# Low-rank inner products moved ahead of the fourth and fifth key tiles, the solve's blocks stored as whole squares, its steps behind the outputs, and another front order on ScalarE

## The chip, the cores and the metric

The kernel runs on one core of one Trainium2 chip. The metric is the device time of one execution in microseconds. Engines: PE (TensorE) multiplies matrices, ACT (ScalarE) evaluates functions and copies, DVE (VectorE) does elementwise work, POOL (GpSimd) does elementwise work and issues DMAs, and SP (SyncE) only issues DMAs. Each engine takes its own instructions in a fixed order; between engines they wait on semaphores.

## The reference, cut to what matters

The program is a two-layer trunk over 512 tokens of width 1024. The change touches only layer 0's time mixing:

```
x_prev = shift(x);  xs = x[None] + (x_prev - x)[None] * mu[:, None, None, :]
r, k, v = einsum('nbtd,nde->nbte', xs[:3], w_rkv)
xw, xa, xg = xs[3], xs[4], xs[5]
w_log = -softplus(-(w0 + tanh(xw @ w1) @ w2)) - 0.5       # low-rank decay
decay = exp(-exp(w_log))
a = sigmoid(a0 + (xa @ a1) @ a2)                          # low-rank rate
g = sigmoid(xg @ g1) @ g2                                 # low-rank gate
kk = k * k_k / |k * k_k|;   k = k * (1 + (a - 1) * k_a)
S = S*w + (S @ -kk)(kk*a)^T + v k^T;  y = S r             # one step per token, 16 heads
```

The layer's channel mixer and the second layer (attention and its channel mixer) follow; they are the same in both kernels.

## The kernel before

The 1024 features lie in eight tiles of 128 partitions, with the 512 tokens in the free dimension. A product of 1024x1024 with the activations is done one output tile (called p) at a time. Each has eight k-steps, and each k-step is three matmuls, since weights and activations are split into a high and a low part: `xh`,`wlo`, then `xl`,`whi`, then `xh`,`whi` (L131 to L135). So one output tile is 24 matmuls of 128x512. A weight arrives by DMA from SP (`wraw`), ACT rounds it to `whi` (L126), and DVE or POOL forms `wlo` (L127).

Time mixing goes through these stages, in this order of code:
- Front: the mean square of x and `rstd` (L145) on ACT as a Ln and an Exp; then `first(k)` per k-step (L434): DVE forms `h`, ACT `hm`, DVE the mixed input, ACT rounds it to `XH[k]`, and DVE forms `XL[k]`.
- Keys (i = 1): `group(1, 0)` runs tiles 0 to 2 with the k-steps interleaved (72 matmuls, `ps_pj`). Then tile 3, the low-rank inner products for k = 0 to 3, tile 4, the inner products for k = 4 to 7 (`inner`, L454), each k with three mixed inputs `lm`, for which ACT makes `lhm`, and three or five plain fp32 matmuls (`ps_l`).
- Low-rank outputs: `hidden` (L401), the gate's sigmoid, then `lora(p)` (L495) beside `group(1, 5)`, which runs tiles 5 to 7. `lora` is four matmuls `ps_lo` and two sigmoids per p.
- Values (i = 2) with `keyed` (L576) in between: `factors` (L516, two Exp per p, `kr` and `ksq`), `key2` (L532, `ps_kn`, Ln and Exp on ACT as `krv`), and `ab` (L542). `ab(p)` makes per chunk and head a 64x64 block and writes it to DRAM as `s_ab`, with two POOL DMAs. Its tile comes from a pool of three buffers with the tag `sq`, shared with `ksq` and `krv`.
- Receptances (i = 0) and the solve: `solve` (L609) loads the triangular 32x32 blocks from `s_ab`, does 31 elimination steps on DVE for the first four chunks (g = 0) and 31 for the last four (g = 1), and writes the inverses to `s_xd` and `s_x1`. `steps(n)` puts n of them at a place in the code, and `fetch_x(ch)` (L653) reads what chunk ch needs.
- The loop over eight chunks (L869): `u_step`, `u2_step`, `scores`, `s_step`, `tokens`, `y_tokens`, `yt`, `inv1`, `inv2`.

A scheduler orders each engine's instructions from the code's order and from priorities (`tc.high_priority`, which weights and solve steps use). `preload_act_table_set` (L94) loads an ACT function table at a fixed place; where a function's table isn't loaded, a load is put in front of it (`ACT_TABLE_LOAD` without that line).

Of the kernel before, what the change touches and what calls it, by code (L numbers as in the profile page):

```python
# [31 lines left out]
SM_SCALE = 1.0 / math.sqrt(96.0)  # L32
LOG_EXP = "natural_log_exp_and_others"
HALF = (slice(0, 64), slice(64, 128))
# [21 lines left out]
class Trunk:  # L56
# [23 lines left out]
    def act(self, out, in_, func=AF.Copy, **kw):  # L80
        self.nc.scalar.activation(out=out, in_=in_, func=func, **kw)  # L81

# [9 lines left out]

    def use_log_exp(self):
        self.tc.keep_in_program_order(self.nc.scalar.preload_act_table_set(LOG_EXP))  # L94

# [49 lines left out]
    def rstd(self, out, ss, n, ps=None):  # L145

        if ps is None:
            ss = ss if isinstance(ss, list) else [ss]
            ps = self.bank("ps_ss")[:, :ss[0].shape[1]]
            for i, s in enumerate(ss):  # L150
                self.nc.tensor.matmul(ps, lhsT=self.ones, rhs=s, start=i == 0, stop=i == len(ss) - 1)  # L151
        self.act(out, ps, AF.Ln, scale=1.0 / n, bias=self.eps)
        self.act(out, out, AF.Exp, scale=-0.5)


    def run(self):
# [4 lines left out]
        dp = self.open("scratch", space=DRAM)  # L161
        self.s_ab = dp.tile([2, DT, 4, P, C], F32, name="s_ab")
        self.s_xd = dp.tile([2, P, D], F32, name="s_xd")
# [143 lines left out]
    def time_mix(self, nxt, cp, gt):  # L307
# [21 lines left out]
        x = self.x  # L329
        self.use_log_exp()  # L330

# [15 lines left out]
        rs = t1.tile([P, T], F32, tag="en", name="rs")  # L347
        self.rstd(rs, None, D, ps)
        def mix(i, k):
            hm = tp.tile([P, T], F32, tag="hm", name="hm", bufs=1)  # L350
            self.act(hm, h[:, k, 1:], AF.Copy, scale=om[:, 8 * i + k:8 * i + k + 1])
            m = tp.tile([P, T], F32, tag="xs", name="xs")
            self.stt(m, h[:, k, 0:T], V("mu", 8 * i + k), hm, ALU.mult, ALU.add)
            self.act(XH[k], m)
            return k, m
# [9 lines left out]

        def group(i, p0, pre=None, prio=GP, mid=None):

            lag = LAG
            w = [self.weight(I["wrkv"][i, p], prio=prio) for p in range(p0, p0 + 3)]
            q = [self.bank("ps_pj") for _ in range(3)]  # L370
            pend = None
            for k in range(DT + 1):
                n = pre(k) if pre and k < DT else k
                if k:
                    if pre:
                        mix_lo(*pend)
# [64 lines left out]

        qk = group(1, 0, first, prio=G0)
        for t, n in ((w1, I["w1"]), (g1, I["g1"]), (self.cst, I["cst"][:, :256]), (self.ident, I["cst"][:, 256:]), (scan, I["scan"])):
# [10 lines left out]
        def inner(k):  # L454
            lm = []
            for i, tag in enumerate(("xs", "be", "kr")):
                hm = tp.tile([P, T], F32, tag="sq", name="lhm", bufs=3)
                self.act(hm, h[:, k, 1:], AF.Copy, scale=om[:, 8 * (3 + i) + k:8 * (3 + i) + k + 1])
                m = tp.tile([P, T], F32, tag=tag, name="lm", bufs=3 if tag == "kr" else None)
                self.stt(m, h[:, k, 0:T], V("mu", 8 * (3 + i) + k), hm, ALU.mult, ALU.add)  # L460
                lm.append(m)
# [33 lines left out]
        def lora(p):  # L495
            if p == DT:
                return
# [6 lines left out]

        qk = group(1, 5, mid=lora)
        for p in range(5, DT):
            kept(p, qk[p - 5])
        self.use_log_exp()

# [6 lines left out]
        def factors(p):  # L516
            cp = cs[:, p, :]
            en = t1.tile([P, T], F32, tag="en", name="en")
            self.act(en, cp, AF.Exp, scale=CD)
            ka = t1.tile([P, T], F32, tag="ka", name="ka")  # L520
            nc.vector.tensor_scalar(out=c3(ka), in0=bk[:, p, :, 0, :], scalar1=V("ka", p), scalar2=om[:, 48 + p:49 + p], op0=ALU.mult, op1=ALU.add)
            self.act(ar[:, p, :, 1, :], c3(cp), AF.Exp, scale=-CD)
            self.tt(ka, ka, en, ALU.mult)
# [77 lines left out]
        LT, X1 = (s4[:, 1].rearrange("q (i p) (o c) -> q i (p o) c", i=2, o=2)[:, i] for i in range(2))  # L601
        abv = self.s_ab.rearrange("g p c (h b j) t -> (g p c h) b j t", h=2, b=2)
        tmp = {"tm": t1.tile([P, 256], F32, tag="ke", name="tm")}

        def load_a(g, A):
            for b in range(2):
                nc.sync.dma_start(out=A[b * 64:b * 64 + 64], in_=abv[g * 64:g * 64 + 64, b, :, b * 32:b * 32 + 32])

        def solve():  # L609
            nc.sync.dma_start(out=lA, in_=abv[:, 0, :, 32:64])  # L610
            load_a(0, sA)
            nc.vector.tensor_copy(out=lX, in_=lA.rearrange("q j i -> q i j"))
            nc.gpsimd.dma_start(out=self.s_lo, in_=lX.rearrange("q a b -> q (a b)"))
# [255 lines left out]
        for ch in range(NCH):  # L869
# [4 lines left out]
            if ch == 0:  # L874
# [71 lines left out]
class FFN:  # L946
# [25 lines left out]
    def run(self, nxt):  # L972
# [11 lines left out]
        for j in range(FT):  # L984
# [358 lines left out]
```

## Time and profile before

| | us |
|---|---|
| median of 3 runs (range) | 1341.83 (1340.74 to 1344.11) |
| the profiled execution | 1340.55 |
| its span, first to last instruction | 1338.8 |
| PE busy | 1294.0 (97%) |
| DVE busy | 807.5 (60%) |
| ACT busy | 695.8 (52%) |
| POOL busy | 250.9 (19%) |

Between its span and its time lie 1.75 us. Busy time is an average over stages with different limits; a stage has to be read by itself. The mean granted TensorE clock is 0.992 of full speed.

### The profile page before, as it was taken

What the parts mean: (1) busy time and instruction counts of PE and PEld (TensorE: products, weight loads), DVE (VectorE), ACT (ScalarE), POOL (GpSimd) and SP (SyncE); (2) the same over time, 40 slices, a digit from 0 to 9 for tenths busy, and PEclk for the clock granted to TensorE, in tenths of its full rate; (3) what the DMA queues carried; (4) which work ended last, traced back from release to release, by engine and by line L of the source; (5) the groups of instructions that cost most, each with busy time, mean ns of one, the idle gap of its engine ahead of it and who ended that gap; (6) DMA issues with size and microseconds to landing.
All of it is one profiled execution on the core that took longest, in us unless ns stands there. A gap on an engine that the chain in (4) does not pass through costs nothing.

```text
span 1338.8 us, 21742 instructions
## 1 busy us (share of the span) xinstructions
PE 1294.0 (97%) x8120; PEld 1063.4 (79%) x8120; DVE 807.5 (60%) x1458; ACT 695.8 (52%) x1313; POOL 250.9 (19%) x237
## 2 busy tenths in 40 slices
PE   7999999989999999999999999999999999999996
PEld 4566687878998888888888978677988888888886
DVE  7669787977787666665233877873765555550003
ACT  6699744677765444443332566664664444433221
POOL 0001423000000000000000051203154444444440
PEclk8999999999999999999999999999999999999998
DMA  6222595344633323333333145332323332333321
GB/s 208 67 73 84 153 259 142 62 121 119 200 108 127 101 96 95 101 96 87 95 95 95 57 113 122 96 83 64 96 95 103 100 96 95 100 93 90 96 79 64
DMA packets 111084, 141.41 MB, mean 106 GB/s; under 512 B 47553, under 2 KB 54593, under 8 KB 110977
## 3 DMA queue, kind: packets, MB, share of 16 engines
q1 hardware_dynamic: 107568, 129.52, 33.3%
q0 software_dynamic: 3408, 10.49, 2.5%
q8 instruction: 64, 1.05, 0.3%
q14 instruction: 44, 0.35, 0.1%
HBM read 120.31 MB, written 12.58 MB: 99 GB/s over the span
## 4 chain that ended last, share of the span: by engine, by line
PE 72%; DVE 6%; ACT 3%; DMA 1%; issue 1%; SPq 0%; ACTq 0%; DVEq 0%
PE ps_in L134 12%; PE ps_in L135 12%; PE ps_in L133 12%; PE ps_out L133 7%; PE ps_out L135 7%; PE ps_out L134 7%; PE ps_o L1205 2%; PE ps_t L1189 1%; PE ps_wo L133 1%; PE ps_wo L135 1%; PE ps_wo L134 1%; PE ps_ss L151 1%; PE ps_dn L134 1%; PE ps_dn L135 1%; PE ps_dn L133 1%
## 5 line engine op out<-in xcount | busy, mean ns | idle before, releaser
L81 ACT ACTIVATE whi<-wraw 128x512 fp32r<-128x512 f32 (+2 forms) x411 | 249.3, 614 | 358.6 <-PE ps_out L135 129.1
L127 POOL TENSOR_TENSOR wlo<-wraw,whi 128x512 fp32r<-128x512 f32 (+2 forms) x168 | 211.9, 1266 | 690.6 <-ACT whi L81 680.1
L133 PE MATMUL ps_in<-xh,wlo 128*128 128x512 f32 (+1 forms) x768 | 286.2, 373 | 0.2 <-DVE wlo L127 0.2
L135 PE MATMUL ps_in<-xh,whi 128*128 128x512 f32 (+1 forms) x768 | 285.3, 372 | 0.0
L134 PE MATMUL ps_in<-xl,whi 128*128 128x512 f32 (+1 forms) x768 | 285.3, 371 | 0.0
L127 DVE TENSOR_TENSOR wlo<-wraw,whi 128x512 fp32r<-128x512 f32 x237 | 160.0, 682 | 108.8 <-ACT whi L81 106.9
L133 PEld LDWEIGHTS ps_in<-xh,wlo 128*128 128x128 f32 x768 | 144.6, 188 | 25.5 <-DVE wlo L127 0.4
L134 PEld LDWEIGHTS ps_in<-xl,whi 128*128 128x128 f32 x768 | 144.6, 188 | 25.4 <-DVE xl L87 0.2
L135 PEld LDWEIGHTS ps_in<-xh,whi 128*128 128x128 f32 x768 | 144.6, 188 | 24.8
L133 PE MATMUL ps_out<-hh,wlo 128*128 128x512 f32 (+1 forms) x396 | 146.8, 371 | 1.3 <-ACT mg L81 1.3
L134 PE MATMUL ps_out<-hl,whi 128*128 128x512 f32 (+1 forms) x396 | 146.2, 369 | 0.0
L135 PE MATMUL ps_out<-hh,whi 128*128 128x512 f32 (+1 forms) x396 | 146.2, 369 | 0.0
L84 DVE TENSOR_TENSOR macc<-macc,msq 128x512 f32<-128x512 f32 (+1 forms) x25 | 15.7, 626 | 126.7 <-ACT msq L81 126.6
L133 PEld LDWEIGHTS ps_out<-hh,wlo 128*128 128x128 f32 x396 | 74.3, 188 | 16.2 <-ACT mg L81 1.9
L87 DVE SCALAR_TENSOR_TENSOR c<-gp,vec,c 128x512 f32<-128x512 f32 x88 | 71.5, 815 | 24.4 <-ACT c L81 23.1
L133 PE MATMUL ps_pj<-xh,wlo 128*128 128x512 f32 x192 | 77.8, 424 | 8.7 <-ACT xh L81 6.7
L135 PEld LDWEIGHTS ps_out<-hh,whi 128*128 128x128 f32 x396 | 74.3, 188 | 14.2
L134 PEld LDWEIGHTS ps_out<-hl,whi 128*128 128x128 f32 x396 | 74.3, 188 | 14.2
L134 PE MATMUL ps_pj<-xl,whi 128*128 128x512 f32 x192 | 77.7, 406 | 0.1
L135 PE MATMUL ps_pj<-xh,whi 128*128 128x512 f32 x192 | 76.8, 402 | 0.0
L84 DVE TENSOR_TENSOR u<-ps_in,row 128x512 f32<-128x512 f32 x44 | 30.4, 690 | 64.1 <-PE ps_in L135 64.1
L84 DVE TENSOR_TENSOR gp<-ps_in,row 128x512 f32<-128x512 f32 x44 | 30.4, 691 | 60.3 <-PE ps_in L135 49.7
(293 smaller groups left out, 2277.6 us busy)
## 6 DMA issues: line engine op xcount, KB each, us to landing
wraw<-in_win SPq DMA_DIRECT2D x176, 256.0 KB, 2.7
wraw<-in_wout SPq DMA_DIRECT2D x80, 256.0 KB, 2.6
wraw<-in_wrkv SPq DMA_DIRECT2D x48, 256.0 KB, 3.0
wraw<-in_wo SPq DMA_DIRECT2D x32, 256.0 KB, 3.0
x<-in_xT SPq DMA_DIRECT2D x16, 256.0 KB, 4.6
wraw<-in_ow SPq DMA_DIRECT2D x16, 256.0 KB, 3.0
s_ab<-ab POOLq DMA_DIRECT2D x16, 128.0 KB, 2.5
s_vt<-vT POOLq DMA_DIRECT2D x8, 256.0 KB, 3.2
```

The source lines that it names most:

```text
L81: self.nc.scalar.activation(out=out, in_=in_, func=func, **kw)
L84: self.nc.vector.tensor_tensor(out=out, in0=a, in1=b, op=op)
L87: self.nc.vector.scalar_tensor_tensor(out=out, in0=a, scalar=s, in1=b, op0=op0, op1=op1)
L127: self.wlo.tensor_tensor(out=l[:, :w], in0=r, in1=h[:, :w].bitcast(F32), op=ALU.subtract)
L133: mm(ps, lhsT=wl, rhs=xh, start=start, stop=False)
L134: mm(ps, lhsT=wh, rhs=xl, start=False, stop=False)
L135: mm(ps, lhsT=wh, rhs=xh, start=False, stop=stop)
L151: self.nc.tensor.matmul(ps, lhsT=self.ones, rhs=s, start=i == 0, stop=i == len(ss) - 1)
L1189: nc.tensor.transpose(out=q[:, o:o + P], in_=pr[i][:, j * P:(j + 1) * P], identity=t.ident)
L1205: nc.tensor.matmul(q[HALF[i], j * P:], lhsT=VT[pr // 4][j][:, c:c + 64], rhs=w, start=j == 0, stop=j == QB - 1)
```

## The change

1. `use_log_exp` becomes `use_table(name)`, which also loads the sigmoid table. The sigmoid table is loaded behind the inner products. The two Exp of `factors` are held behind the later load of the Ln/Exp table.
2. All eight `inner(k)` stand directly behind the first three key tiles. Tiles 3 and 4 follow, then `lora(0)` and `lora(1)`, then `group(1, 5)` with `lora(k + 2)`.
3. In the front, the weights of key tiles 1 and 2 are issued behind `rstd`'s Exp, and `lhm` is held behind the second `XH`.
4. `s_ab` has the two 32-column halves outermost, so that a 32x32 block is contiguous: four POOL DMAs for each p with rows of 128 B, where there were two with rows of 256 B. The solve's loads read contiguous 4 KB per partition instead of 32 pieces of 128 B. Their order changes, and the transposing copy of the off-diagonal blocks (`lX`) moves from DVE to ACT.
5. In the chunk loop, `steps` are 10, 10, 10 behind `yt` (they were 11, 11, 40 ahead of `y_tokens`), and the rest stands behind chunk 3's `u2_step`. `fetch_x(n)` moves from the end of one round to behind the next round's `u2_step`.

```diff
-        qk = group(1, 0, first, prio=G0)
+        qk = group(1, 0, first, prio=G0, after=normed)
...
-                self.act(hm, h[:, k, 1:], AF.Copy, scale=om[:, 8 * (3 + i) + k:8 * (3 + i) + k + 1])
+                with tc.issue_after(rounded[1].ins):
+                    self.act(hm, h[:, k, 1:], AF.Copy, scale=om[:, 8 * (3 + i) + k:8 * (3 + i) + k + 1])
...
-        for p in range(3, 5):
-            kept(p, proj(1, p))
-            for k in range(4):
-                inner(4 * (p - 3) + k)
+        for k in range(DT):
+            inner(k)
+        kept(3, proj(1, 3))
...
+        self.use_table(SIGMOID)
...
-        qk = group(1, 5, mid=lora)
+        q4 = proj(1, 4)
+        for p in range(2):
+            lora(p)
+        kept(4, q4)
+        qk = group(1, 5, mid=lambda k: lora(k + 2))
...
-        self.use_log_exp()
+        exps = self.use_table()
...
+            with tc.issue_after(exps.ins):
+                self.act(en, cp, AF.Exp, scale=CD)
...
             for g in range(2):
-                nc.gpsimd.dma_start(out=self.s_ab[g, p].rearrange("c q t -> q c t"), in_=c3(o)[:, 4 * g:4 * g + 4])
+                for b in range(2):
+                    nc.gpsimd.dma_start(out=self.s_ab[b, g, p].rearrange("c q t -> q c t"), in_=c3(o)[:, 4 * g:4 * g + 4, 32 * b:32 * b + 32])
...
-            nc.sync.dma_start(out=lA, in_=abv[:, 0, :, 32:64])
             load_a(0, sA)
-            nc.vector.tensor_copy(out=lX, in_=lA.rearrange("q j i -> q i j"))
+            nc.sync.dma_start(out=lA, in_=abv[1, :, 0])
+            self.act(lX, lA.rearrange("q j i -> q i j"))
...
             u2_step(ch, u)
+            if ch == 3:
+                steps(40)
+            if 0 < ch and n < NCH:
+                fetch_x(n)
...
-            if ch < 3:
-                steps((11, 11, 40)[ch])
             y_tokens(ch, q)
             if ch > 0:
                 yt(ch - 1)
+            if ch < 3:
+                steps(10)
...
-            if n + 1 < NCH:
-                fetch_x(n + 1)
```

How the instructions stand on the engines follows at three places. First ACT's order in the front, from `rstd`'s Ln (`rs<-ps_x`) to the first rounded key input `xh`; `whi` are rounded weights. Before:

```order
L81 ACTIVATE rs<-ps_x,eps 128x512
L81 ACTIVATE whi<-wraw 128x512 x2
L81 ACTIVATE rs<-rs 128x512
L81 ACTIVATE hm<-h,om 128x512
L81 ACTIVATE whi<-wraw 128x512 x2
L81 ACTIVATE lhm<-h,om 128x512
L81 ACTIVATE xh<-xs 128x512
```

With the change, the same stretch as far as the second `xh`:

```order
L81 ACTIVATE rs<-ps_x,eps 128x512
L81 ACTIVATE rs<-rs 128x512
L81 ACTIVATE whi<-wraw 128x512 x2
L81 ACTIVATE hm<-h,om 128x512
L81 ACTIVATE whi<-wraw 128x512
L81 ACTIVATE xh<-xs 128x512
L81 ACTIVATE whi<-wraw 128x512
L81 ACTIVATE hm<-h,om 128x512
L81 ACTIVATE xh<-xs 128x512
```

Two roundings moved behind the Exp, and one rounding behind the first `xh` and the `lhm` behind the second.

Next ACT's order where the Ln/Exp table is loaded (`ACT_TABLE_LOAD` of L94), at the end of the keys; `bk<-ps_pj` is `kept`, `en` an Exp, and `ksq` what `ps_kn` multiplies. Before:

```order
L81 ACTIVATE bk<-ps_pj 128x8x64
L94 ACT_TABLE_LOAD
L81 ACTIVATE en<-cs 128x512
L81 ACTIVATE kr<-bk,vec 128x512
L81 ACTIVATE ksq<-bk,vec 128x512
L81 ACTIVATE xh<-xs 128x512
```

With the change, the first `kr` and `ksq` stand among the sigmoids `sg` and `bk<-ps_lo`, 24 rows ahead of that load:

```order
L81 ACTIVATE bk<-ps_lo,vec 128x8x64
L81 ACTIVATE kr<-bk,vec 128x512
L81 ACTIVATE sg<-ps_lo,vec 128x512
L81 ACTIVATE bk<-ps_lo,vec 128x8x64
L81 ACTIVATE ksq<-bk,vec 128x512
L81 ACTIVATE sg<-ps_lo,vec 128x512
```

So `kr` and `ksq` of p = 0 no longer follow the table load.

Last POOL's order over the last writes of `s_ab` (p = 3 to 7); `s_v` and `s_vt` are the values. Before:

```order
L551 DMA s_ab<-ab 128x4x64 x2
L432 DMA s_v<-vv 128x4x128
L423 DMA s_vt<-vT 128x512
L551 DMA s_ab<-ab 128x4x64 x2
L432 DMA s_v<-vv 128x4x128
L551 DMA s_ab<-ab 128x4x64 x6
```

With the change:

```order
L564 DMA s_ab<-ab 128x4x32 x3
L436 DMA s_v<-vv 128x4x128
L564 DMA s_ab<-ab 128x4x32
L427 DMA s_vt<-vT 128x512
L564 DMA s_ab<-ab 128x4x32 x4
L436 DMA s_v<-vv 128x4x128
L564 DMA s_ab<-ab 128x4x32 x12
```

POOL issues four writes for each p where it issued two, and twelve in a row at the end where there were six.

## Rows read from the trace of the kernel before

**Rows 1.** The page: PE's busy tenths in 40 slices of the span

```profile
PE   7999999989999999999999999999999999999996
```

**Rows 2.** Stretches: length, busy PE, PEld, DVE, ACT, POOL, PEclk, DMA, GB/s

```profile
10.00:20.00 10.00, 3.72 (x9) 1.74 (x8) 8.03 (x15) 8.08 (x14) 0.00 (x0) 0.87 0.87 298
20.00:30.00 10.00, 9.76 (x34) 7.02 (x32) 9.29 (x16) 5.26 (x10) 0.00 (x0) 0.78 0.23 79
30.00:70.00 40.00, 39.75 (x148) 20.14 (x148) 27.51 (x43) 28.35 (x46) 0.00 (x0) 1.00 0.22 67
70.00:100.00 30.00, 27.68 (x115) 20.72 (x113) 21.34 (x28) 29.68 (x48) 0.00 (x0) 1.00 0.25 79
100.00:110.00 10.00, 8.20 (x25) 5.79 (x26) 9.24 (x16) 10.00 (x18) 0.00 (x0) 0.83 0.07 26
...
160.00:230.00 70.00, 69.54 (x372) 54.75 (x371) 59.24 (x128) 31.99 (x51) 19.24 (x32) 1.00 0.72 200
230.00:350.00 120.00, 110.59 (x2048) 100.48 (x2045) 93.69 (x199) 81.92 (x184) 1.67 (x4) 0.99 0.46 118
600.00:620.00 20.00, 20.00 (x90) 16.54 (x89) 12.22 (x19) 7.64 (x12) 0.00 (x0) 1.00 0.33 89
```

**Rows 3.** PE's waits to 400 us: line, released by: total us, times, longest

```profile
PE ps_pj L133 <- ACT xh L81: 6.7, 2, 6.3
...
PE ps_kn L534 <- ACT ksq L81: 2.4, 1, 2.4
PE ps_ab L547 <- ACT krv L81: 2.3, 1, 2.3
PE ps_i L669 <- DMA s<-s_xd: 2.3, 1, 2.3
```

**Rows 4.** ACT in time in the front: start, us, instruction, idle before it

```profile
12.78 1.14 ACT L81 ACTIVATE whi<-wraw 128x512 fp32r<-128x512 f32 x2
...
15.42 0.72 ACT L81 ACTIVATE hm<-h,om 128x512 f32<-128x512 f32 x1 [0.99 <-DVE h L87]
16.05 1.13 ACT L81 ACTIVATE whi<-wraw 128x512 fp32r<-128x512 f32 x2
...
17.71 0.61 ACT L81 ACTIVATE xh<-xs 128x512 fp32r<-128x512 f32 x1
```

**Rows 5.** PE in time: end of the inner products, first `ps_kn`, first `ps_ab`

```profile
69.27 1.05 PE L470 MATMUL ps_l<-lm,ar 128*32 128x512 f32 x4
...
101.80 1.12 PE L534 MATMUL ps_kn<-ksq,cst 128*128 128x512 f32 x2 [2.43 <-ACT ksq L81]
...
116.73 0.56 PE L547 MATMUL ps_ab<-ar,bk 64*64 64x64 f32 x10
```

**Rows 6.** ACT in time: one table load between neighbours, and the first `krv`

```profile
77.05 0.63 ACT L81 ACTIVATE gs<-gs 32x512 f32<-32x512 f32 x1
77.70 1.28 ACT L81 ACT_TABLE_LOAD   x1
79.00 0.63 ACT L81 ACTIVATE ar<-cs 128x512 f32<-128x512 f32 x1
...
112.32 0.61 ACT L81 ACTIVATE krv<-krv 128x512 f32<-128x512 f32 x1
```

**Rows 7.** POOL in time: the first, fourth and last pair of `s_ab` writes

```profile
121.12 1.69 POOL L551 DMA_DIRECT2D s_ab<-ab  x2 [119.15 <-ACT ab L81]
...
145.81 1.49 POOL L551 DMA_DIRECT2D s_ab<-ab  x2 [0.35 <-ACT ab L81]
...
163.06 1.49 POOL L551 DMA_DIRECT2D s_ab<-ab  x2 [2.16 <-ACT ab L81]
```

**Rows 8.** ACT in time: the wait for an `s_ab` landing

```profile
150.45 0.69 ACT L81 ACTIVATE krv<-ps_kn,tiny 128x512 f32<-128x512 f32 x1 [2.20 <-DMA s_ab<-ab]
```

**Rows 9.** DMA issues: queue, count, KB each, median us to landing

```profile
s_ab<-ab POOLq DMA_DIRECT2D x16, 128.0 KB, 2.5
...
s<-s_ab SPq DMA_DIRECT2D x4, 256.0 KB, 4.4
```

More of the change, by code (lines that the diff above doesn't have):

```diff
@@ L32 @@
 SM_SCALE = 1.0 / math.sqrt(96.0)
-LOG_EXP = "natural_log_exp_and_others"
+LOG_EXP, SIGMOID = "natural_log_exp_and_others", "sigmoid_and_others"
 HALF = (slice(0, 64), slice(64, 128))
@@ L80, in act @@
     def act(self, out, in_, func=AF.Copy, **kw):
-        self.nc.scalar.activation(out=out, in_=in_, func=func, **kw)
+        return self.nc.scalar.activation(out=out, in_=in_, func=func, **kw)
     def tt(self, out, a, b, op):
@@ L91, in split, with use_table @@
         self.tt(lo, src, hi.bitcast(F32), ALU.subtract)
-    def use_log_exp(self):
-        self.tc.keep_in_program_order(self.nc.scalar.preload_act_table_set(LOG_EXP))
+    def use_table(self, name=LOG_EXP):
+        return self.tc.keep_in_program_order(self.nc.scalar.preload_act_table_set(name))
     def bank(self, nm):
@@ L152, in rstd @@
         self.act(out, ps, AF.Ln, scale=1.0 / n, bias=self.eps)
-        self.act(out, out, AF.Exp, scale=-0.5)
+        return self.act(out, out, AF.Exp, scale=-0.5)
     def run(self):
@@ L161, in run @@
         dp = self.open("scratch", space=DRAM)
-        self.s_ab = dp.tile([2, DT, 4, P, C], F32, name="s_ab")
+        self.s_ab = dp.tile([2, 2, DT, 4, P, 32], F32, name="s_ab")
         self.s_xd = dp.tile([2, P, D], F32, name="s_xd")
@@ L329, in time_mix @@
         x = self.x
-        self.use_log_exp()
+        self.use_table()
         warm = bank2("ps_w")
@@ L347, in time_mix @@
         rs = t1.tile([P, T], F32, tag="en", name="rs")
-        self.rstd(rs, None, D, ps)
+        normed = self.rstd(rs, None, D, ps)
+        rounded = []
         def mix(i, k):
@@ L353, in mix @@
             self.stt(m, h[:, k, 0:T], V("mu", 8 * i + k), hm, ALU.mult, ALU.add)
-            self.act(XH[k], m)
+            rounded.append(self.act(XH[k], m))
             return k, m
@@ L364, in proj, with group @@
             return q
-        def group(i, p0, pre=None, prio=GP, mid=None):
+        def group(i, p0, pre=None, prio=GP, mid=None, after=None):
             lag = LAG
-            w = [self.weight(I["wrkv"][i, p], prio=prio) for p in range(p0, p0 + 3)]
+            w = [self.weight(I["wrkv"][i, p0], prio=prio)]
+            with tc.issue_after(after.ins) if after else ExitStack():
+                w += [self.weight(I["wrkv"][i, p], prio=prio) for p in range(p0 + 1, p0 + 3)]
             q = [self.bank("ps_pj") for _ in range(3)]
@@ L495, in lora @@
         def lora(p):
-            if p == DT:
+            if p >= DT:
                 return
@@ L503, in lora @@
             self.act(bk[:, p, :, 0, :], c3(q), AF.Sigmoid, bias=V("a0", p))
-        qk = group(1, 5, mid=lora)
+        q4 = proj(1, 4)
[3 more added lines that the diff above has]
+        qk = group(1, 5, mid=lambda k: lora(k + 2))
         for p in range(5, DT):
             kept(p, qk[p - 5])
-        self.use_log_exp()
+        exps = self.use_table()
         def before(p):
@@ L518, in factors @@
             en = t1.tile([P, T], F32, tag="en", name="en")
-            self.act(en, cp, AF.Exp, scale=CD)
+            with tc.issue_after(exps.ins):
+                self.act(en, cp, AF.Exp, scale=CD)
             ka = t1.tile([P, T], F32, tag="ka", name="ka")
             nc.vector.tensor_scalar(out=c3(ka), in0=bk[:, p, :, 0, :], scalar1=V("ka", p), scalar2=om[:, 48 + p:49 + p], op0=ALU.mult, op1=ALU.add)
-            self.act(ar[:, p, :, 1, :], c3(cp), AF.Exp, scale=-CD)
+            with tc.issue_after(exps.ins):
+                self.act(ar[:, p, :, 1, :], c3(cp), AF.Exp, scale=-CD)
             self.tt(ka, ka, en, ALU.mult)
@@ L601, in time_mix @@
         LT, X1 = (s4[:, 1].rearrange("q (i p) (o c) -> q i (p o) c", i=2, o=2)[:, i] for i in range(2))
-        abv = self.s_ab.rearrange("g p c (h b j) t -> (g p c h) b j t", h=2, b=2)
+        abv = self.s_ab.rearrange("b g p c (h a j) t -> b (g p c h) a j t", h=2, a=2)
         tmp = {"tm": t1.tile([P, 256], F32, tag="ke", name="tm")}
@@ L606, in load_a @@
             for b in range(2):
-                nc.sync.dma_start(out=A[b * 64:b * 64 + 64], in_=abv[g * 64:g * 64 + 64, b, :, b * 32:b * 32 + 32])
+                nc.sync.dma_start(out=A[b * 64:b * 64 + 64], in_=abv[b, g * 64:g * 64 + 64, b])
         def solve():
-            nc.sync.dma_start(out=lA, in_=abv[:, 0, :, 32:64])
             load_a(0, sA)
-            nc.vector.tensor_copy(out=lX, in_=lA.rearrange("q j i -> q i j"))
+            nc.sync.dma_start(out=lA, in_=abv[1, :, 0])
+            self.act(lX, lA.rearrange("q j i -> q i j"))
             nc.gpsimd.dma_start(out=self.s_lo, in_=lX.rearrange("q a b -> q (a b)"))
@@ L1004, in run @@
             ls.append(b)
-        t.use_log_exp()
+        t.use_table()
         mp = t.open("mg")
```

## The prediction

> **What bounds the kernel now.** I read the page's slices first. PE is at 9 tenths in nearly every slice [rows 1], and in the stretch 600:620 it is busy for all 20 us with 90 matmuls, so one costs 20/90 = 0.222 us there [rows 2]. From about 400 us on nothing but fewer matmuls could shorten the program, and the change takes no matmul away. So I cut the first 400 us into stretches [rows 2]. PE is short of work in the front (3.72 of 10 us), in 70:100 (27.68 of 30), in 100:110 (8.20 of 10) and in the chunk loop, 230:350 (110.59 of 120). ACT has no time left where PE is short: 29.68 of 30 us in 70:100, 10.00 of 10 in 100:110. That is the stage of the low-rank outputs and their sigmoids. The granted clock falls to 0.83 in 100:110, and to 0.87 and 0.78 in the two front stretches, which is the lower level (1.2 of 2.4 GHz) for a part of each, behind PE's longest stops. PE's waits give the names [rows 3]: the first `xh` (6.3 us), `ksq` (2.4 us, in front of the first `ps_kn` at 101.80 [rows 5]), `krv` (2.3 us), and the fetch from `s_xd` for chunk 4 (2.3 us).
>
> **The front.** The change lets 1.14 us of rounding (the two `whi` at 12.78) follow the Exp instead of standing ahead of it [rows 4]. `hm` at 15.42 had waited 0.99 us for `h`, which needs that Exp, so the 1.14 counts in full. Behind `hm` one of two roundings (half of 1.13, so 0.57) and an `lhm` (the 0.53 between the end of those roundings at 17.18 and `xh` at 17.71) move behind `xh`. Together 2.24 us. Against it, DVE now has two `wlo` between `h` and the mixed input; with the front's DVE rows (9.29 us busy for 16 instructions, 0.58 each [rows 2]) they cost up to 1.16. That leaves about 1.1, and PE starting earlier also shortens the stretch at the lower clock a little: I take -1.3 us. The bounds are 0 (DVE, at 9.29 of 10, hands the loss to the later k-steps) and -3: the 2.24 in full and part of the 2.2 us that a clock of 0.78 over 20:30 costs.
>
> **The inner products in one piece.** Their own time I leave as it is: in 30:70, where before's stand with a key tile between the halves, PE is busy 39.75 of 40 us, ACT 28.35 and DVE 27.51 [rows 2], so PE paces them. The cover for `lm` is now the inner products alone. A miss here would cost up to 1 us; I take 0.
>
> **From the end of the inner products to the first `ps_ab`.** This carries the forecast. Before, it runs from 69.27 + 1.05 = 70.3 to 116.73 [rows 5], 46.4 us, in which PE does 127 key and value matmuls and 32 `ps_lo`. With the change tiles 3 and 4 also stand behind the inner products, and the first `ps_ab` stands two matmuls earlier: 173 and 32, so 46 more. Had they been done elsewhere at full pace, before would take 46.4 + 46 x 0.222 = 56.6 us for the same work. If PE is the limit, the changed stretch takes 205 x 0.222 = 45.5, and 1.1 for the two first `ps_kn` [rows 5], so 46.6 us: a gain of 10.0. If ACT is the limit, its new order has 60 operations and three table loads as far as the last key tile's `kept`, and 12 operations and one load from there to the first `krv`'s Exp. An operation takes 0.56 us: 29.68 less three loads of 1.28 and the 0.96 of a fourth that began before 70, over the other 45 [rows 2, 6]. So 72 x 0.56 + 4 x 1.28 = 45.4. Behind it DVE needed 3.8 us, from the end of the first `krv`'s Exp at 112.93 [rows 6] to `ps_ab` at 116.73 [rows 5]. That makes 49.2 us: a gain of 7.4. The two limits are close, and ACT's is the later one. I take -7.4. The wait for `ksq` and the lower clock in 100:110 are inside it: `ksq` now stands ahead of the table load, so it is early, and what is late next is `krv` in front of the first `ps_ab`, priced by ACT's sum. As bounds I take -10.0, and -4 if ACT in addition idles as DVE's or PE's turn comes (it then gains only the 2.4 us wait, its 1.7 us of lost clock and nothing in 70:100).
>
> The row on the table load [rows 6]: the operation ahead of it ends at 77.68, the load starts at 77.70 and takes 1.28, and the next operation starts at 79.00. The Trainium skill ("ScalarE: Activation LUTs", section "What ACT_TABLE_LOAD costs") adds a drain of 1.38 us to such a load, 2.66 in all. By that the four loads would cost ACT 5.5 us more, and the gain of the stretch would be 1.9. By the row, which shows no drain, it is 7.4; the sum goes by the row.
>
> **`s_ab` as squares.** Each p now has four writes from POOL; a pair took 1.49 us [rows 7], so the last write starts 1.5 us later. That is hidden where `ab` tiles are rare, and before's pairs come (163.06 - 121.12)/7 = 6.0 us apart on average [rows 7], later ones closer. It isn't hidden at the fourth: written at 145.81, it held ACT's `krv` for 2.20 us until 150.45 [rows 7, 8], and PE's wait of 2.3 us for `krv` follows from that [rows 3]. So I take +1.5, once. Bounds: 0, if ACT and PE come there later by their own work, and +3, if the wait behind the fifth tile's writes adds the same again. In exchange the solve's loads have whole rows; they took 4.4 us in 128 B pieces [rows 9]. DVE's first solve steps now stand ahead of the last `xl` of the receptances, so sooner loads are needed there; in 160:230 PE is busy 69.54 of 70 us and has no loss to give back [rows 2]. The moved transposing copy goes to ACT, busy 31.99 of those 70: nothing.
>
> The Trainium skill ("DMA: Bandwidth & Descriptors", section "Specifications") says that transfers below 512 B leave the line rate, since they are done as read-modify-write. By it the new 128 B writes would land later than the 256 B ones, whose median is 2.5 us [rows 9]. The nearest row of 128 B pieces is the solve's load, 4.4 us for four times the bytes of a new write [rows 9]; by the bytes a write is then no later than before, and the sum keeps 1.5.
>
> **The chunk loop.** The solve's last step for the later chunks stands three DVE operations further back; at 93.69/199 = 0.47 us each [rows 2] that is 1.4 us on the way to `s_xd` and to PE's wait of 2.3 us [rows 3]. The solve's faster start works the other way. I take +0.5, bounds -2.3 (the wait goes) and +2. Fetching later changes nothing for chunks 1 to 3, whose blocks are long in DRAM; for chunks 4 and on SP waited for `s_xd` anyway.
>
> **The sum.** -1.3 - 7.4 + 1.5 + 0.5 = -6.7 us. The profiled execution took 1340.55: its span 1338.8 and 1.75 around it. So 1333.85 in its terms; the median of the runs is 1.28 higher, and the forecast is 1335.1.
>
> **The rivals.** A: ACT stays the bound and the gain is mostly used up. The low-rank stretch gives only 4, the front 0.5, and the squares take 2.5 (their bound nearly): -2.0, and 1339.8. For it: ACT at 29.68 and 10.00, and its new order holds more operations as far as `kept` than PE's matmuls cover. The table load's drain, by the page named above, would end here too (1.9 - 1.5 - 0.5 + 1.3 = 1.2 us gained). Against it: the row shows no drain. B, slower: the squares pace the stage. One `ab` copy (0.56), four issues (3.0) and a landing (2.5) make 6.1 us from one tile to the next, against the 6.0 on average before; with a landing like the fourth's (145.81 + 1.49 to 150.45, so 3.15 us) 6.7. If the chain holds PE's order over all seven steps from one tile to the next, each later by the 1.5 us of issues and by the 0.65 that such a landing takes longer, this costs 7 x 2.15 = 15.1 us; the front and the low-rank stretch give 8.7, the loop loses 0.5: +6.9, 1348.7. It decides once every write takes over 3 us to land. Against it: before's first pairs have more room than the last ones. C: PE is the limit throughout, -2 - 10.0 + 0.5 for the squares and 0 for the loop: -11.5, 1330.3. For it: ACT and PE lie only 2.6 us apart in my sums, and the earlier start of the sigmoids may carry over to the later tiles.
>
> **How the numbers follow.** I give the forecast 0.50, with a range of its own of 1332 to 1338.5, A 0.23, B 0.10, C 0.17. What a measurement tells from no change is 0.3%, 4.0 us: faster is below 1337.8, slower above 1345.9. Nine tenths of the forecast, all of C and a little of A lie below: 0.64. The rest of the forecast, the most of A and some of B lie between: 0.27. Slower is 0.09. The range that should hold 8 in 10 goes from 1329.5 (C and half a microsecond) to 1343 (A, and the squares' other bound and the loop's on top); it leaves out B and the tails.
>
> **What would show it.** In the changed profile the first `xh` should start near 16.4 instead of 17.71. The first `ps_kn` should wait for nothing, and the granted clock should stay at 1.00 from there to the first `ps_ab`. From the end of the inner products to that `ps_ab` it should be about 49 us; 54 or more means rival A. One of ACT's operations should wait longer than 2.2 us for `s_ab`, and PE's wait for `krv` should grow to 3 or 4 us; waits at several tiles mean B. PE's wait for `s_xd` should be 2 to 4 us. I am wrong at the root if PE's loss in the low-rank stretch is not ACT's doing: if ACT shows idle time there and PE still waits.

## The result and the profile after

The changed kernel takes 1350.27 us (median of 5 runs, 1347.03 to 1350.97), the kernel before beside it on the same chip 1340.74 (median of 5, 1338.59 to 1344.11). The ratio is 1.0067, with a 95% interval of 1.0053 to 1.0082: slower, where a gain of 6.7 us was forecast, and outside the range. The profiled execution took 1349.0, its span 1347.2.

The stretches of the changed kernel, to be laid beside [rows 2] (same columns):

```profile
10.00:20.00 10.00, 5.19 (x12) 2.65 (x11) 7.88 (x15) 6.98 (x12) 0.00 (x0) 0.75 0.92 313
20.00:30.00 10.00, 9.51 (x36) 6.90 (x36) 9.84 (x17) 7.49 (x14) 0.00 (x0) 0.90 0.20 67
30.00:70.00 40.00, 40.00 (x144) 18.91 (x143) 29.37 (x47) 32.63 (x51) 0.00 (x0) 1.00 0.17 53
70.00:100.00 30.00, 28.41 (x123) 22.43 (x122) 24.27 (x32) 29.14 (x51) 0.00 (x0) 1.00 0.31 101
100.00:110.00 10.00, 9.99 (x41) 7.23 (x39) 9.72 (x17) 9.90 (x19) 0.00 (x0) 1.00 0.20 71
110.00:130.00 20.00, 17.59 (x151) 12.96 (x152) 16.16 (x29) 15.86 (x35) 6.59 (x9) 1.00 0.27 70
130.00:160.00 30.00, 25.07 (x191) 18.88 (x192) 18.82 (x31) 19.82 (x37) 16.69 (x24) 0.94 0.54 145
160.00:230.00 70.00, 66.51 (x347) 52.68 (x349) 55.35 (x121) 31.61 (x48) 22.19 (x34) 0.98 0.67 199
230.00:350.00 120.00, 108.08 (x2002) 97.04 (x2002) 91.58 (x196) 79.64 (x175) 4.24 (x8) 0.96 0.42 103
```

Two stretches of the kernel before that were not looked at ahead of the prediction:

```profile
110.00:130.00 20.00, 19.46 (x132) 14.56 (x132) 19.05 (x32) 18.72 (x35) 3.87 (x6) 1.00 0.30 94
130.00:160.00 30.00, 27.14 (x258) 20.24 (x257) 22.02 (x36) 23.60 (x49) 12.58 (x18) 1.00 0.53 158
```

Up to 110 us the change does what it was forecast to do: PE gains in 10:20 and 70:110, and the clock of 0.83 in 100:110 is 1.00. Behind that PE, DVE and ACT are all less busy than before in 110:160, which points to something that isn't an engine. PE alone is busy 1.87 + 2.07 us less there, 3.03 less in 160:230 and 2.51 in 230:350, and its mean granted clock is lower from 130 us on (0.94, 0.98 and 0.96 in the last three stretches). PE's longest waits up to 420 us name the later places:

```profile
PE ps_i L682 <- DMA s<-s_xd: 6.2, 1, 6.2
PE ps_pj L133 <- ACT xh L81: 5.3, 3, 4.8
PE ps_ab L558 <- DVE bk L84: 5.2, 2, 2.9
PE ps_bo L709 <- DVE rkk L87: 3.5, 1, 3.5
```

Against [rows 3] the wait for `ksq` is gone and the first is 1.5 us shorter; the wait for `s_xd` has grown from 2.3 to 6.2, and two names are new.

To see where each microsecond goes I compared when the same matmul (the n-th onto a named tile) starts in two traces. Start minus its start in the kernel before, us; the experiments' columns are described below. `ps_vt` belongs to the values, `ps_bo` to the receptances (it multiplies `rkk`, their product with the keys), `ps_sc` to the loop's scores, and `ps_ss` is the first matmul behind the loop:

| matmul | before, at | after | old blocks (e1) | old steps (e2) | both old (e3) |
|---|---|---|---|---|---|
| first `ps_pj` | 18.37 | -1.3 | -2.0 | -1.3 | -1.2 |
| last inner product `ps_l` | 69.73 | -9.7 | -10.4 | -9.7 | -9.6 |
| first `ps_ab`, p = 0 | 116.73 | -5.9 | -6.6 | -4.5 | -5.8 |
| first `ps_ab`, p = 6 | 157.18 | +2.7 | -7.3 | +4.6 | -6.3 |
| last `ps_vt` | 183.62 | +0.4 | -8.2 | +2.4 | -7.2 |
| last `ps_bo` | 226.99 | +5.1 | -6.7 | +4.1 | -4.9 |
| `ps_sc` of chunk 4 | 273.56 | +5.1 | -4.8 | +4.8 | -5.6 |
| first `ps_ss`, past the wait for `s_xd` | 361.34 | +9.0 | -0.8 | +4.0 | -4.8 |

(The last inner product is early because 48 key matmuls now stand behind it.) So the changed kernel arrives at the key/value outputs 5.9 us ahead and loses in three places: 8.6 us between the outputs of p = 0 and p = 6, 4.7 from the last `ps_vt` to the last `ps_bo` of the receptances, and 3.9 at chunk 4's wait for `s_xd`.

The table also shows how far a single trace can be trusted. The changed kernel and e2 run the same instructions in the same order on each engine as far as 260 us, e1 and e3 as far as 250 us, and yet each pair differs by up to 2 us in a row up to there. The first loss is far above that: 8.6 and 9.1 us (e2), where e1 and e3 gain 0.7 and 0.5. The second is not: 4.7 in the changed kernel, but 1.8 in e2, and 1.5 and 2.3 with the old blocks.

**The first place.** POOL and ACT of the changed kernel in time, at the first two tiles (as [rows 7, 8]):

```profile
116.50 3.46 POOL L564 DMA_DIRECT2D s_ab<-ab  x4 [114.53 <-ACT ab L81]
...
127.98 3.00 POOL L564 DMA_DIRECT2D s_ab<-ab  x4 [0.97 <-ACT ab L81]
```

```profile
123.98 0.69 ACT L81 ACTIVATE krv<-ps_kn,tiny 128x512 f32<-128x512 f32 x1 [3.74 <-DMA s_ab<-ab]
...
133.54 0.69 ACT L81 ACTIVATE krv<-ps_kn,tiny 128x512 f32<-128x512 f32 x1 [1.46 <-DMA s_ab<-ab]
```

`ab` and `krv` share three buffers. The four issues begin at 116.50 and the `krv` that takes a buffer next isn't written until 123.98, 7.5 us later: 2.7 until the fourth issue begins, and 4.7 until that write has landed (the median of all these writes is 2.7). Before, the only such wait came at the fourth pair [rows 8]; now the first tile has one, and what stands behind `krv` inherits it: DVE's `bk`, and PE, which waits 2.24 and 2.02 us:

```profile
128.21 1.15 PE L558 MATMUL ps_ab<-ar,bk 64*64 64x64 f32 x32 [2.24 <-DVE bk L84]
...
134.28 1.86 PE L433 MATMUL ps_vt<-cen,vT 128*128 128x128 f32 x8 [2.02 <-ACT krv L81]
```

**The second place.** ACT, DVE and PE of the changed kernel at the first receptance:

```profile
177.91 2.04 ACT L81 ACTIVATE s<-s 128x1024 f32<-128x1024 f32 x1 [1.45 <-DMA s<-s_ab]
```

```profile
180.50 0.69 DVE L84 TENSOR_TENSOR xl<-xs,xh 128x512 fp32r<-128x512 f32 x1 [2.37 <-ACT xh L81]
...
192.51 0.42 DVE L84 TENSOR_TENSOR s<-s,tm 128x252 f32<-128x252 f32 x1
192.85 0.68 DVE L84 TENSOR_TENSOR ar<-ps_pj,ar 128x512 f32<-128x512 f32 x1
...
194.65 0.75 DVE L87 SCALAR_TENSOR_TENSOR rkk<-ar,vec,bk 128x512 f32<-128x512 f32 x1
```

```profile
195.54 1.61 PE L709 MATMUL ps_bo<-rkk,cst 128*128 128x512 f32 x2 [3.49 <-DVE rkk L87]
```

DVE takes its work in order, and the solve's steps stand ahead of the product `ar`: 18 of them here, two operations each, where the kernel before has 13 and the old blocks 12. Twelve of the 18 also start late: DVE stood idle for 2.37 us until ACT had made the last `xh`, and ACT had first waited 1.45 us for the load of the moved transposing copy (`s<-s`) and copied for 2.04. PE stops for 3.49 us and then runs partly at the lower clock: the two `ps_bo` take 1.61 (1.10 before), and the granted clock is 0.83 in 190:200.

**The third place.** The solve's last step reaches POOL, and PE, so late:

```profile
284.74 0.57 POOL L642 DMA_DIRECT2D s_xd<-s  x1 [48.99 <-issue]
```

```profile
294.17 1.12 PE L682 MATMUL ps_i<-s 128*64 128x64 f32 x16 [6.19 <-DMA s<-s_xd]
```

Before, that write was issued at 276.81.

### The profile page after: what moved, and what is told of

It reads as the page before. It is cut to its first block, busy times and chain, and to the rows that moved or that the text cites. A ratio compares the mean times of both kernels' runs of the same rounds, so it can differ in the third digit from the quotient of the medians.

```text
span 1347.2 us, 21781 instructions
## 1 busy us (share of the span) xinstructions
PE 1297.6 (96%) x8120; PEld 1066.6 (79%) x8120; DVE 806.7 (60%) x1457; ACT 696.8 (52%) x1313; POOL 263.2 (20%) x253
## 4 chain that ended last, share of the span: by engine, by line
PE 71%; DVE 3%; ACT 2%; DMA 1%; issue 1%; SPq 0%; POOL 0%; ACTq 0%; POOLq 0%; DVEq 0%
PE ps_in L134 12%; PE ps_in L135 12%; PE ps_in L133 12%; PE ps_out L133 7%; PE ps_out L135 7%; PE ps_out L134 7%; PE ps_o L1220 1%; PE ps_wo L133 1%; PE ps_wo L135 1%; PE ps_wo L134 1%; PE ps_t L1204 1%; PE ps_ss L151 1%; PE ps_dn L134 1%; PE ps_dn L135 1%; PE ps_dn L133 1%
```

## The experiments

Ratios are to the kernel before, run beside each on the same chip, with 95% intervals.

### Which part costs: blocks and steps undone apart and together

Theory S lays the loss on the square blocks, theory L on the steps behind the outputs. e1 puts the old `s_ab` with its two writes, its loads and the copy on DVE back into the changed kernel; e2 the old place of the steps and of the fetch; e3 both.

```diff
 e1
-self.s_ab = dp.tile([2, 2, DT, 4, P, 32], F32, name="s_ab")
+self.s_ab = dp.tile([2, DT, 4, P, C], F32, name="s_ab")
...
-for b in range(2):
-    nc.gpsimd.dma_start(out=self.s_ab[b, g, p]..., in_=c3(o)[:, 4 * g:4 * g + 4, 32 * b:32 * b + 32])
+nc.gpsimd.dma_start(out=self.s_ab[g, p]..., in_=c3(o)[:, 4 * g:4 * g + 4])
 e2
-if ch == 3: steps(40)          # behind u2_step
-if 0 < ch and n < NCH: fetch_x(n)
...
+if ch < 3: steps((11, 11, 40)[ch])
 y_tokens(ch, q)
-if ch < 3: steps(10)           # behind yt
...
+if n + 1 < NCH: fetch_x(n + 1) # behind inv2
```

> The changed kernel with part 4 undone: s_ab written with two DMAs of 256 B rows for each p, the solve's loads and the transposing copy on DVE as before. Against the kernel before, the changed one loses 9 us: it is 5.9 us ahead at the first ps_ab, 2.7 behind at p = 6, 5.1 behind at the first ps_bo, 9.0 behind after chunk 4's wait for s_xd. Theory S (the doubled writes): ACT's waits for s_ab landings shrink from 3.7 + 1.5 us to under 1, PE is still 3 or more ahead at p = 6, the wait of 3.5 us in front of ps_bo goes too since the DVE order has the receptances earlier, and the run takes 1339 or less. Theory P (the ring of three buffers is too short for the new, earlier order, whatever the writes): the waits shrink by 1.5 us each, PE is level or behind at p = 6, and the run takes 1344 to 1347.

Measured: 1340.79, ratio 1.0002 [0.9991, 1.0012].

> The changed kernel with part 5 undone: steps 11, 11, 40 ahead of y_tokens and fetch_x(n + 1) at the end of a round. Theory L (the loop's order sets the s_xd wait): PE's wait for s_xd falls from 6.2 us to about 2.3 and the run is 4 us shorter, 1346. Theory H (the solve is handed over late by the stages ahead): the wait only falls by the three DVE operations, 1.4 us, and the run takes 1348 to 1350.

Measured: 1346.14, ratio 1.0037 [1.0021, 1.0052].

> Parts 4 and 5 undone, so only the front order, the inner products in one piece, and the table loads are new. If my prediction's two gains are real (front 1.3 us, 5.9 us ahead at the first ps_ab) and keep, theory S says 1334 to 1336. Theory P says the lead is used up at the later ab tiles by the ring: 1339 to 1342.

Measured: 1336.16, ratio 0.9960 [0.9946, 0.9973].

With the medians of the changed kernel the four make a square: the blocks cost 9.5 us with the new steps (1350.3 - 1340.8) and 10.0 with the old (1346.1 - 1336.2), the steps 4.1 and 4.6. Both theories hold, and the costs add. Theory P, three buffers too few whatever the writes, is out as the whole cause: with the old writes PE is 7.3 and 6.3 us ahead at p = 6. (What e1 undoes is all of part 4: the writes, the loads, their order and the copy on ACT.) e1 missed its expected time because the late solve cost more there than I thought; PE's waits for `s_xd` in e1, e2 and e3, one kernel each:

```profile
PE ps_i L681 <- DMA s<-s_xd: 7.3, 1, 7.3
```

```profile
PE ps_i L682 <- DMA s<-s_xd: 2.4, 1, 2.4
```

```profile
PE ps_i L681 <- DMA s<-s_xd: 3.1, 1, 3.1
```

and ACT's waits for `s_ab` between 100 and 180 us in e2 and e3:

```profile
ACT krv L81 <- DMA s_ab<-ab: 9.7, 3, 4.3
```

```profile
ACT ab L81 <- DMA s_ab<-ab: 0.7, 1, 0.7
ACT krv L81 <- DMA s_ab<-ab: 0.2, 1, 0.2
```

The blocks go with ACT's wait, the steps with PE's. What is left without both is a gain: e3 is the rest of the change, and its median is 4.5 us below that of the kernel before (1336.16 against 1340.67).

### What in the blocks costs: the buffer, the issues or the rows

If the wait for a buffer carries the loss, a fourth buffer gives it back. e4 is the whole change with `bufs=4` for that tag.

```diff
-o = tp.tile([P, T], F32, tag="sq", name="ab", bufs=3)
+o = tp.tile([P, T], F32, tag="sq", name="ab", bufs=4)
```

> The whole change, with four buffers of the tag sq instead of three, so that an ab tile's buffer is wanted one allocation later. Theory P: ACT's waits for s_ab (3.7, 1.5 us) go nearly altogether, PE keeps its lead of 5 us at p = 4 and 3 or more at p = 6, and the run takes 1341 to 1344 (the losses at ps_bo and s_xd stay). Theory S says the same of the waits, since it also needs the ring; if the waits stay although a buffer is free, the cause is another one (POOL's issue time itself, or ACT's order).

Measured: 1343.6, ratio 1.0016 [1.0007, 1.0025], 6.7 us below the changed kernel's median. The last `ps_vt` comes 2.1 us before its old time instead of 0.4 after. The waits of ACT come at other tiles and the longest is shorter, but in all they are 5.3 us, against 5.4 in the changed kernel:

```profile
ACT krv L81 <- DMA s_ab<-ab: 2.7, 1, 2.7
ACT ab L81 <- DMA s_ab<-ab: 2.6, 2, 2.4
```

By the expectation, waits that stay speak for POOL's issue time or ACT's order instead. Still PE loses 3.0 us from p = 0 to p = 6 instead of 8.6. But e4 changes more than the buffer: the inner products' `lhm` has the same tag, and from 22 us on ACT runs another order, with the last inner product 1.2 us ahead of the changed kernel's. How much of the 6.7 us the buffer gives by itself is not shown.

e5 has square blocks in two writes (one for each half of the columns, over all 8 chunks), with the old steps: as many issues as before, twice the rows of half the length (its load of `lA` is cut in two as well). e6 has the old blocks in four writes, two chunks each: as many rows as before in twice the issues.

```diff
 e5, on e2
-    nc.gpsimd.dma_start(out=self.s_ab[b, g, p]..., in_=c3(o)[:, 4 * g:4 * g + 4, 32 * b:32 * b + 32])
+    nc.gpsimd.dma_start(out=self.s_ab[b, p].rearrange("g c q t -> q (g c) t"), in_=c3(o)[:, :, 32 * b:32 * b + 32])
 e6, on e3
-nc.gpsimd.dma_start(out=self.s_ab[g, p]..., in_=c3(o)[:, 4 * g:4 * g + 4])
+for b in range(2):
+    c = slice(4 * g + 2 * b, 4 * g + 2 * b + 2)
+    nc.gpsimd.dma_start(out=self.s_ab[g, p, 2 * b:2 * b + 2]..., in_=c3(o)[:, c])
```

> As e2 (old steps, the new square blocks), but each p writes its squares with two DMAs, one per 32-column half over all eight chunks: 1024 rows of 128 B each, so twice the rows in all that the old blocks had, with two issues. e2 took 1346.1 and e3, with old blocks, 1336.2. Theory I (the count of issues: each holds POOL 0.75 us and the last starts 1.5 us later): 1336 to 1339, and ACT's waits for s_ab under 1.5 us. Theory R (the 128 B rows, twice as many, land later): 1344 to 1347, waits of 3 us or more, and a POOL issue or a landing visibly longer than the old pair's 0.75 and 2.5 us. Between, both count.

Measured: 1346.1, ratio 1.0043 [1.0029, 1.0057].

> As e3 (old blocks, old steps), but each pair of writes is cut into four, of two chunks each, with the old 256 B rows. Theory I: 1343 to 1346, like e2. Theory R: 1336 to 1338, like e3.

Measured: 1338.55, ratio 0.9986 [0.9974, 0.9998].

By the medians the doubled issues alone cost 2.4 us (e6 against e3), the doubled rows alone 9.9 (e5), and both 10.0 (e2). The traces share it out otherwise. From p = 0 to p = 6, e3 gains 0.5 us and e7, which runs the same orders (see below), loses 1.8; e6 loses 4.1, e5 4.6, e2 9.1 and the changed kernel 8.6. There issues and rows each cost, by about as much. e5 then loses 7.1 from the last `ps_vt` to the last `ps_bo` (PE waits 4.7 us for `rkk`). It has 18 steps ahead of `ar` like e2, and ACT waited 4.6 us for a landing of `s_vt` in front of the last `xh`; whether that comes from the rows is not shown. With one trace for each, these shares are rough.

The issue of the writes on POOL in ns (min/median/max), for the changed kernel, e5 and e6, and then, in the same order, the KB of a write and the median us to its landing:

```profile
L564 POOL DMA_DIRECT2D s_ab<-ab x32: 752/752/1033, 116.5 to 168.1; - x32
```

```profile
L563 POOL DMA_DIRECT2D s_ab<-ab x16: 885/893/1067, 116.6 to 162.8; - x16
```

```profile
L565 POOL DMA_DIRECT2D s_ab<-ab x32: 706/723/877, 116.6 to 163.6; - x32
```

```profile
s_ab<-ab POOLq DMA_DIRECT2D x32, 64.0 KB, 2.7
```

```profile
s_ab<-ab POOLq DMA_DIRECT2D x16, 128.0 KB, 3.3
```

```profile
s_ab<-ab POOLq DMA_DIRECT2D x32, 64.0 KB, 2.2
```

128 KB in 1024 rows of 128 B land in 3.3 us, where 512 rows of 256 B needed 2.5 [rows 9]; 64 KB land in 2.7 us in rows of 128 B and in 2.2 in rows of 256 B. The Trainium skill ("DMA: Bandwidth & Descriptors", section "Specifications") puts transfers below 512 B off the line rate; that takes in both lengths and names no step between them, and these rows show one. So a tile's time from `ab` to free buffer has both parts, four issues and a later landing, and neither theory is right alone.

### What in the steps costs: their place, and DVE's order

e7 has the old blocks, the steps back in their old place, and only the fetch where the change put it. e9 is the whole change with 12 solve steps ahead of the first receptance product instead of 18.

```diff
 e7, on e1
-if ch == 3: steps(40)
...
+if ch < 3: steps((11, 11, 40)[ch])
 y_tokens(ch, q)
...
 e9
-steps(2)
+steps(2 if k < 6 else 0)
...
-steps((0, 0, 0, 5, 5, 4, 0, 0)[p])
+with tc.issue_after(first_r[0].ins):   # behind the first product ar
+    steps((0, 0, 6, 5, 5, 4, 0, 0)[p])
```

> As e1 (old blocks), with the steps 11, 11, 40 ahead of y_tokens as before, but fetch_x(n) left behind the next round's u2_step. e1 took 1340.8, e3 1336.2. If the steps' places make the difference: 1336 to 1337, and PE's wait for s_xd about 3 us, as in e3. If the fetch's place does: 1340 to 1341 and a wait of about 7 us, as in e1.

Measured: 1336.51, ratio 0.9969 [0.9959, 0.9980], no different from e3; PE waits 2.7 us for `s_xd`. Against e1, where only the steps differ, it is 4.3 us less: the place of the steps costs. The fetch's place isn't tested by itself, for in the traces every engine of e7 runs e3's instructions in e3's order. So e7 is e3 measured a second time. Its profiled run (1339.74) is the slowest of its nine, and its trace stands 2.5 us behind e3's at the last `ps_vt` and 3.9 behind past the wait for `s_xd`.

> The whole change, with only 12 of the solve's steps in front of the first receptance product instead of 18 (rmid issues none from k = 6 on, and the rest is held behind that product). The changed kernel waits 3.5 us for rkk in front of ps_bo and falls from 3.0 to 5.1 us behind there. If the 18 steps on DVE are the cause: no such wait over 1 us, PE 0 to 1 us behind at the last ps_bo, 1345 to 1346, unless the steps left for the chunk loop lengthen the wait for s_xd by as much (then 1348 to 1350). If the late xl or the copy on ACT is the cause: no change, 1350.

Measured: 1347.88, ratio 1.0056 [1.0041, 1.0070]. The median is 2.4 us below the changed kernel's, less than expected, and the intervals overlap. The mechanism shows in the trace: the first `ps_bo` of e9 waits for nothing,

```profile
192.10 1.02 PE L709 MATMUL ps_bo<-rkk,cst 128*128 128x512 f32 x2
```

and the last one stands at +0.2 us instead of +5.1. (The profiled run is e9's fastest, 1345.25; the medians' 2.4 us is the better price.) PE's wait for `s_xd` stays at 6.2, so the third loss doesn't come from the second. The copy on ACT has a part of its own: e2 has the same 18 steps as the changed kernel, but its copy waits 0.4 us for the load instead of 1.45, and PE waits 2.2 us for `rkk` instead of 3.5. No run puts back the copy alone.

### What the front is worth

e10 is the kernel before with the front's new order alone, e11 is e3 without it.

```diff
 e10, on the kernel before
-qk = group(1, 0, first, prio=G0)
+qk = group(1, 0, first, prio=G0, after=normed)
...
-self.act(hm, h[:, k, 1:], AF.Copy, scale=...)
+with tc.issue_after(rounded[1].ins):
+    self.act(hm, h[:, k, 1:], AF.Copy, scale=...)
 e11, on e3: the same lines the other way
```

> The kernel before with the front order alone (weights of key tiles 1 and 2 behind the Exp, lhm behind the second rounded input). My prediction priced it at -1.3 us; the changed kernel's first ps_pj stands 1.3 us earlier. If it keeps: 1339.4. If DVE hands it back in the next k-steps: 1340.7.

Measured: 1340.23, ratio 1.0002 [0.9990, 1.0013].

> As e3 (old blocks, old steps) without the front order: the inner products in one piece and the table loads alone. e3 took 1336.2. If the gains add: 1337.5 (the front's 1.3 less), so the low-rank part alone gives 3 to 3.5 of the 4.5 us.

Measured: 1337.13, ratio 0.9969 [0.9957, 0.9982]; e3's interval overlaps it.

The front's microsecond arrives and is not kept. In e10 the lead is 1.1 us at the first `ps_pj`, 0.7 at `ps_sc` of chunk 4 and 0.2 past the wait for `s_xd` (2.5 us there): the solve sets that point, and PE only comes to it earlier and waits longer.

### A version that beats both

e8 is e3 with four buffers; e12 is e8 with e9's order and the solve's block `sA` loaded ahead of `lA`.

```diff
 e12, on e8
-nc.sync.dma_start(out=lA, in_=abv[:, 0, :, 32:64])
 load_a(0, sA)
+nc.sync.dma_start(out=lA, in_=abv[:, 0, :, 32:64])
...
+with tc.issue_after(first_r[0].ins):   # as e9
```

> e3 with four buffers of the tag sq. If the ring still costs with two writes a pair (e3's ACT waits 0.9 us for s_ab, PE 1.5 us for krv): 1334 to 1335.5. If the ring matters only with four writes: 1336, no change against e3.

Measured: 1335.94, ratio 0.9957 [0.9944, 0.9970]: no different from e3, whose ACT waits only 0.9 us in all for `s_ab`.

> e8 (front, inner products in one piece, tables, four buffers; old blocks and steps in the loop), with the solve loading its diagonal blocks first, as the change does, and the steps held behind the first receptance product as in e9. In e3 DVE waits 1.9 us for the solve's blocks and PE 2.5 us at ps_bo. If that is a loss that can be had back: 1333 to 1335; if the solve's later steps take it back at s_xd: 1336 or more.

Measured: 1335.14, ratio 0.9961 [0.9948, 0.9975]. Faster than both kernels, and not to be told from e3 or e8.

## Why the prediction was wrong

**The step that failed** is the pricing of the squares: "So I take +1.5, once", and behind it "in 160:230 PE is busy 69.54 of 70 us and has no loss to give back". Measured by e1 and e3 the blocks cost 9.5 to 10.0 us against +1.5, bounds 0 and +3. I charged the extra issues at the one tile where [rows 8] shows a wait, and took the others' 6.0 us between pairs as room. But that average counts from pair to pair, and what must fit is from `ab` to the next writer of its buffer: 7.5 us now at the first tile, and from p = 0 to p = 6 alone 8.6 us were lost. The nearest row for the landing, the loads' 4.4 us for four times the bytes, was no guide to a write: at equal bytes the short rows added 0.8 us (3.3 against 2.5).

**That PE was busy all through 160:230 was no reason to expect no loss there.** It said that the order on DVE was right before. The change moved five more steps ahead of the first product, and 4.7 us went in this trace, 1.8 in e2's with the same order; e9 gets 2.4 of them back by the medians. The moved copy, priced at "nothing" since ACT is half idle there, stood ahead of the last `xh` on an engine that works in order, and waited for its load. I saw that DVE's first steps had moved, and asked only what they need, not what stands behind them.

**Rival B** named the mechanism, with its price 1.6 us off the measured median (1348.7 against 1350.27), but that agreement is partly luck. Its seven equal losses along the stage aren't there: 8.6 us are lost from p = 0 to p = 6, and 2.3 come back up to the last `ps_vt`, so 6.3 in place of its 15.1. The other 8.8 are about what the receptances and the loop lost, 4.7 and 3.9, for which B has 0.5. Its point of decision, every write over 3 us, wasn't reached either (median 2.7); the buffer's wait is issues and landing together. It had 0.10; [rows 8], a wait for the very buffer whose writes were to double, spoke for more.

**The chunk loop** was mis-sized: +0.5 forecast, bound +2; the place of the steps costs 4.1 to 4.6 us by the medians, 3.9 at the wait itself. "Three DVE operations further back" counts operations on DVE; the step's write was issued 7.9 us later than before (284.74 against 276.81), of which PE was itself 5.1 late.

**The front** was right where it was priced: the first `xh` starts as forecast, and the first `ps_pj` gains 1.29. ACT and PE of the changed kernel, for [rows 4] and [rows 3]:

```profile
16.40 0.63 ACT L81 ACTIVATE xh<-xs 128x512 fp32r<-128x512 f32 x1 [0.51 <-DVE xs L87]
```

```profile
17.08 1.22 PE L133 MATMUL ps_pj<-xh,wlo 128*128 128x512 f32 x2 [4.81 <-ACT xh L81]
```

What failed is carrying it into the sum: by e10 and e11 no gain at the end can be measured.

**The inner products in one piece** were taken at 0, a miss at 1. At the last one, -1.29 and 48 matmuls at 0.222 (10.66) would make -11.95; it stands at -9.67, so 2.3 us were lost. About 1.0 of them shows in rows of its own (below). Most of it goes with the front's order: e11, without it, has its first `ps_pj` at +0.74, would come to -9.92 by the same sum, and stands at -9.42, 0.5 lost. What holds the rest stays open, with PE busy throughout.

**From the inner products to the first `ps_ab`** the forecast held. PE of the changed kernel, for [rows 5]:

```profile
60.58 0.50 PE L133 MATMUL ps_pj<-xh,wlo 128*128 128x512 f32 x1
...
103.30 1.02 PE L545 MATMUL ps_kn<-ksq,cst 128*128 128x512 f32 x2
...
110.83 0.67 PE L558 MATMUL ps_ab<-ar,bk 64*64 64x64 f32 x14
```

From 60.58 to 110.83 are 50.25 us; 49.2 were forecast, and 56.6 would be no gain. So 6.4 of 7.4. `ps_kn` waits for nothing and the clock is 1.00 in 100:110. That fits ACT as the limit, by whose sum it was forecast: it is busy 29.14 of 30 us and 9.90 of 10. But PE is then nearly as full (28.41 and 9.99), so the rows don't tell the two limits apart. Its table load, for [rows 6]:

```profile
97.48 0.59 ACT L81 ACTIVATE bk<-ps_pj 128x512 f32<-128x512 f32 x1
98.08 1.28 ACT L94 ACT_TABLE_LOAD   x1
99.37 0.64 ACT L81 ACTIVATE en<-cs 128x512 f32<-128x512 f32 x1
```

The load starts 0.01 us behind its neighbour and the next operation 0.01 behind the load. The Trainium skill ("ScalarE: Activation LUTs", section "What ACT_TABLE_LOAD costs") adds a drain of 1.38 us; here too the trace shows none.

Of the signs I gave for being wrong, "waits at several tiles mean B" and a wait for `s_xd` above 4 us are what came; PE's wait for `krv` did not grow (2.0 us, from 2.3), since the delay reached PE through `bk` as well. Of the 8.7 us forecast for the front and the low-rank part about half is real: without the squares and the moved steps the change gives 4.5 us by the medians (e3). Those two cost 14.1 (1350.27 - 1336.16), more than all of it.

## What to carry to other kernels

When a change lengthens a transfer out of a rotating buffer, time the loop from the write of the buffer to its next writer, for the first turn as well as for the mean, and put the issues and the landing into it. A stretch in which an engine never waits has an order that happens to fit: ask of each instruction moved ahead of others on an in-order engine who waits for those others. And look for the point downstream that something else sets (here the solve's write): a gain ahead of it counts only as far as that point moves too. Before a trace is read to the microsecond, look for two runs whose engines have the same order, and see how far they differ.

## What the hardware showed that was not expected

**Halves that run beside each other.** PE of the changed kernel, in the first two rounds of the inner products:

```profile
37.54 1.07 PE L469 MATMUL ps_l<-lm,ar 128*64 128x512 f32 x2
38.55 0.50 PE L134 MATMUL ps_pj<-xl,whi 128*128 128x512 f32 x1
...
42.20 0.64 PE L469 MATMUL ps_l<-lm,ar 128*64 128x512 f32 x1
42.20 0.64 PE L470 MATMUL ps_l<-lm,ar 128*64 128x512 f32 x1
42.68 0.59 PE L469 MATMUL ps_l<-lm,ar 128*64 128x512 f32 x1
42.68 0.59 PE L470 MATMUL ps_l<-lm,ar 128*64 128x512 f32 x1
43.21 1.13 PE L471 MATMUL ps_l<-lm,ar 128*128 128x512 f32 x2
```

Side by side, the two products of 64 columns take PE 1.01 us together (42.20 to 43.21). In the first round key matmuls stand between them, and each takes that long alone (37.54 to 38.55): 1.0 us more.

**Issues cost by their number.** POOL takes 0.72 us (median) for 64 KB in 256 rows (e6), 0.75 for 64 KB or 128 KB in 512 rows (the changed kernel; before), 0.89 for 128 KB in 1024 rows (e5): splitting a write in two nearly doubles its issue time.

**Whole rows gained the loads nothing.** The solve's loads in the changed kernel, for [rows 9]:

```profile
s<-s_ab SPq DMA_DIRECT2D x4, 256.0 KB, 4.3
```

With whole rows of a square they land in 4.3 us, in 128 B pieces they took 4.4. What the squares were to buy was not there, at this size and beside the other transfers of this stage (the DMA engines are busy 0.67 of 160:230, before 0.72).
